# Two blocks on one core: an early table load, the split of the router's logits, and where sums of squares are issued

## The chip, the cores and the metric

The program runs on one core of one Trainium2 chip. A core has a matrix engine (TensorE, PE), a vector engine (VectorE, DVE), a scalar engine (ScalarE, ACT), a general engine (GpSimd, POOL) and a synchronising engine (SyncE, SP) that issues most transfers. Engines run side by side, each one in the order of its own instruction list, and wait for one another by semaphores. ScalarE and GpSimd issue transfers from their own lists too. The metric is device time in microseconds of one launch; shown is the median of three runs. One execution with a profile is looked at beside it.

## The reference, cut to what matters

256 tokens of width 1024 go through two blocks in float32.

- Block 1 has two layers. Each: x += (gated sum of a dilated attention and a convolution branch with layer norm and silu) @ w_out; then x += mixture of experts: `lg = h @ w_rg`, `le = h @ w_re` (4 groups of 8 experts: the best group, in it the best two experts per token), `silu(h @ w_gate[e]) * (h @ w_up[e]) @ w_down[e]`; then x += sigmoid(rms_norm(x) @ w_ple_gate) * (p @ w_ple_proj). In front of each part x is normalised: `x * rsqrt(mean(x*x) + 1e-6) * g`. At the end of block 1 comes a last such norm.
- Block 2 has one layer. It begins with `rmsnorm(x) @ w_in`, whose first columns u go through a causal convolution of four taps, then through block-diagonal products (gates of a linear recurrence); the gated linear unit, an attention with compressed, selected and windowed keys, and an MLP follow.

Since the scale of a norm is one number per token, the kernel multiplies with it late: it transposes x at once, multiplies by the gain g only, and applies the root of the mean square to the products.

## The kernel before, in words

**Tiles and numbers.** x lies in the on-chip memory as two tiles of 128 tokens by 1024. A weight block of 128 rows by 1024 comes from memory into one of four buffers (raw); ScalarE rounds it to the matrix engine's short format (whi, L304), VectorE subtracts to get the rest (wlo, L272), in one of three buffers each; PE multiplies the parts in three products (L267). Activations are split in the same way. Sums lie in eight banks, four of them for such products, four for other uses (aux).

**Turns.** `turn` (L398) transposes x for some of its eight groups of 128 channels by PE (L405) and copies the result with the gain: either to a plain tile, one group by VectorE (L410) and one by ScalarE (L412), or split in two parts, by ScalarE (L414) and VectorE (L415). `self.turned` is the last transpose.

**Sums of squares.** `sq_part` (L356) has ScalarE square a piece of x and add it up (L367), for each of the two token tiles. `ssq` and `rstd` add the pieces (L374, L353) and take the power -1/2 on GpSimd (L354). `row_sb` (L388) spreads such a root over all partitions: VectorE makes dg (L384), PE multiplies it, ScalarE copies it to rB (L390).

**Route.** In `route` the logits of a layer's 36 outputs are summed over eight groups k of channels (L697). `logits(range(KR))` is issued as it stands; the rest only behind `self.turned`, the last transpose. With KR = 2 the first two groups are issued ahead. Then comes the selection on VectorE (L704 to L721), and the gathering of tokens.

**Expert tail.** The last experts' outputs are added to x in five chunks of channels (`CHUNKS`, L911); behind each chunk stands a turn with norm_ple's gain, and, when 256 columns are done, the sum of squares of these (L984). `ple_k` multiplies the turned groups by w_ple_gate. `after` (from L998) takes tanh of the products with the root rh as scale (L1010), multiplies (L1011), adds to x (L1013), and turns x with the next norm's gain for the layer that follows. Behind this loop x is multiplied by the last norm's gain in layer 1 (yf, L1027), and both x and yf are squared and summed (L1028, `final_norm`).

**Start of block 2.** u's product is drained by VectorE, which multiplies by rB (L1139) and convolves (L1140, L1142). Since the recurrence wants another split over partitions, each pair of channel groups goes out to memory from ScalarE's list (sx, L1149 and L1154) and comes back in (xr, L1163), also from ScalarE's list, one transfer for each of four blocks; ScalarE and VectorE split xr (xh and xl, L280, L281) and PE multiplies. ScalarE's other work there: the casts of the next weight blocks (L304), tanh for gelu of the second gate (L1211, yg) and its table.

**What sets the order.** A list scheduler orders each engine's instructions by a simulated timeline (`schedule_with_timeline_sim`). `tc.issue_after(i)` holds instructions made inside it until i has been placed. A DMA issued from an engine's list waits behind what stands in front of it there.

Of the kernel before, what the change touches and what calls it, by code (L numbers as in the profile page):

```python
# [11 lines left out]
F32 = mybir.dt.float32  # L12
# [3 lines left out]
AF = mybir.ActivationFunctionType  # L16
# [5 lines left out]
P = 128  # L22
# [25 lines left out]
RING0, RING1 = 15, 20  # L48

BG, BGH = 4, 5  # L50
KR = 2
NG1 = 2
NY = 1
RQ = lambda nc: nc.scalar
# [164 lines left out]
class Kern:  # L219
# [178 lines left out]
    def turn(self, src, gcol, dst=None, kps=(0, 1, 2, 3), kds=None):  # L398

        nc = self.nc  # L400
        for kds in [kds] if kds else [(2 * kp, 2 * kp + 1) for kp in kps]:
            ps = self.ps(self.aux)
            for j, kd in enumerate(kds):
                for tt in range(2):
                    self.turned = nc.tensor.transpose(ps[:, j * T + tt * P:j * T + (tt + 1) * P], src[:, tt, kd * P:(kd + 1) * P], self.ident)  # L405
            for j, kd in enumerate(kds):
                pj, g = ps[:, j * T:(j + 1) * T], self.vec[:, gcol + kd:gcol + kd + 1]
                if dst is not None:
                    if j == 0:
                        nc.vector.tensor_scalar_mul(dst[:, kd, :], pj, g)  # L410
                    else:
                        nc.scalar.activation(dst[:, kd, :], pj, AF.Copy, scale=g)  # L412
                else:
                    nc.scalar.activation(self.hT[0][:, kd, :], pj, AF.Copy, scale=g)  # L414
                    nc.vector.scalar_tensor_tensor(self.hT[1][:, kd, :], pj, g, self.hT[0][:, kd, :].bitcast(F32),  # L415
                                                   op0=ALU.mult, op1=ALU.subtract)


    def setup(self):
        nc, a, cp = self.nc, self.a, self.cp  # L420
        self.x = cp.tile([P, 2, D], F32, name="x")
        xs = a["x"][0].rearrange("(t p) d -> p t d", p=P)
        for i in range(4):
            nc.sync.dma_start(self.x[:, :, i * 256:(i + 1) * 256], xs[:, :, i * 256:(i + 1) * 256])
        cst = cp.tile([P, C_COLS], F32, name="cst")
        nc.scalar.dma_start(cst[:, :2 * P], a["consts"][:, :2 * P])
        self.vec = cp.tile([P, a["vec"].shape[1]], F32, name="vec")
        nc.scalar.dma_start(self.vec, a["vec"])
        self.cst = cst
        self.ident = cst[:, C_ID:C_ID + P]  # L430
        self.J = cst[:, C_J:C_J + P]
        self.cos = cst[:, C_COS:C_COS + T]
        self.sin = cst[:, C_SIN:C_SIN + T]
        self.mask = cst[:, C_MASK:C_MASK + 3 * P]
        self.tri = cst[:, C_TRI:C_TRI + P]
        self.ones = cst[:, C_ONE:C_ONE + P]
        self.iota = cst[:, C_IOTA:C_IOTA + CAP]
        self.iota1 = cst[:, C_IOTA + 1:C_IOTA + 1 + CAP]
        self.act_h = lambda j, k: self.hT[j][:, k, :]
        self.nhalf = cp.tile([P, 32], F32, name="nhalf")  # L440
        nc.vector.memset(self.nhalf, -0.5)
        self.ones512 = cp.tile([P, P], F32, name="ones512")
        nc.vector.memset(self.ones512, 1.0 / 512.0)
        self.rv = cp.tile([RW, a["rv"].shape[1]], F32, name="rv")
        self.nv = cp.tile([P, a["nv"].shape[1]], F32, name="nv")
        self.spc = cp.tile([RW, 5, RC], F32, name="spc")

        g = VEC["norm_mix_2", 0]
        gf = VEC["norm_final", 0]
        nc.vector.tensor_tensor(self.vec[:, g:g + KD], self.vec[:, g:g + KD], self.vec[:, gf:gf + KD], op=ALU.mult)  # L450

        for l in range(DEPTH):
            w0 = VEC["w_dw", l]
            nc.vector.tensor_scalar_mul(self.vec[:, w0:w0 + 4 * CK], self.vec[:, w0:w0 + 4 * CK], 0.5)
            g0 = VEC["ln_conv_g", l]
            nc.vector.tensor_scalar_mul(self.vec[:, g0:g0 + 8], self.vec[:, g0:g0 + 8], 0.5)
# [213 lines left out]
    def route(self, l, mp):  # L670
# [25 lines left out]
        def logits(ks):  # L696
            for k in ks:  # L697
                for tt in range(2):
                    self.mm(pls[tt][:, :36], self.xT[:, k, tt * P:(tt + 1) * P], wr[:, k, :], k == 0, k == KD - 1)
        logits(range(KR))  # L700
        with self.tc.issue_after(self.turned.ins):
            logits(range(KR, KD))
        for tt in range(2):
# [209 lines left out]
    def moe_ple(self, l):  # L913
        nc, tc, a = self.nc, self.tc, self.a
        self.npiece, self.gates, self.ny = 0, (), 0
        with tc.tile_pool(name=f"m1_{l}", bufs=1) as mp:
# [7 lines left out]
            def ple_k(kks, after=None):  # L924
                last = None
                for hf in range(2):
                    kp = kks[0] // 2
                    if (kp, hf) not in wvs:
                        wvs[kp, hf] = self.wload(("w_ple_gate", l, hf * 512, 2 * kp), 2)
                    wv = wvs[kp, hf]  # L930
                    with tc.issue_after(last.ins) if after and last else ExitStack():
                        for tt in range(2):
                            for kk in kks:
                                for n, (j, i) in enumerate(((0, 0), (0, 1), (1, 0))):
                                    last = self.mm(pss[hf][tt], self.hT[j][:, kk, tt * P:(tt + 1) * P], wv[i][:, kk % 2, :],
                                                   kk == 0 and n == 0, kk == KD - 1 and n == 2)
                    if after is not None:
                        after(hf, last)
# [34 lines left out]
            c0, prev = 0, None  # L973
            for i, cw in enumerate(CHUNKS):
                kds = range(c0 // P, (c0 + cw) // P)
                self.quad_out(hds, c0, cw, self.aux)
                if i == 0:

                    self.new_hT(self.slot)
                    pss.extend([self.ps() for i in range(2)] for j in range(2))  # L980
                self.turn(self.x, VEC["norm_ple", l], kds=kds)
                c0 += cw
                if c0 % 256 == 0:
                    self.sq_part(c0 // 256 - 1, self.x, c0 - 256, 256)  # L984

                if prev is not None:
                    ple_k(prev)
                prev = kds
# [32 lines left out]
            for hf in range(2):  # L1021
                for c in range(2):
                    n = 512 * (2 * hf + c)
                    xs = self.x[:, :, n // 2:n // 2 + 256]
                    if end:

                        nc.vector.tensor_tensor(self.yf[:, :, n // 2:n // 2 + 256], xs, self.gf[:, n // 2:n // 2 + 256].unsqueeze(1).to_broadcast([P, 2, 256]), op=ALU.mult)  # L1027
                self.sq_part(hf, self.x, hf * 512, 512)  # L1028
            if end:
                ssx = self.ss  # L1030
                for hf in range(2):
# [550 lines left out]
```

## Time and profile before

| what | us |
|---|---|
| median of 3 runs | 1885.41 |
| lowest, highest | 1883.4, 1886.54 |
| profiled execution | 1890.22 |
| its span | 1888.3 |
| PE busy | 1588.2 (84%) |
| VectorE busy | 850.1 (45%) |
| ScalarE busy | 581.9 (31%) |
| GpSimd busy | 58.3 (3%) |
| mean granted clock of PE | 0.917 of full |

The span is read by stages. Layer 0's mixer runs to 197 us and its route to 206; the experts' weights are then streamed, to about 640; tail and layer 1's mixer follow to 855, layer 1's experts to 1300, the tail to 1345, and block 2 to the end. Busy shares are means over stages that have different limits, so the rows below are taken from single places.

### The profile page before, as it was taken

The numbers are of one execution on the slowest core, as the hardware profiler recorded it, in microseconds if no ns is written. First come the engines' busy times: TensorE is split into PE (matmuls) and PEld (weight loads), VectorE is DVE, ScalarE is ACT, GpSimd is POOL, SyncE is SP. The second block draws the span as 40 slices with busy tenths as digits, with TensorE's granted clock in tenths as the row PEclk, the third lists the DMA queues.
The fourth block names the chain that finished last, engine by engine and source line by source line (L and its number), as shares of the span: only waits on it lengthen the run. The fifth ranks groups of instructions, "written<-read, shape, count | busy, mean of one in ns | idle before, by whom it ended". The sixth has DMA issues, their size and how long they took to land. (4 is left out here: it accounts for less than half of the span.)

```text
span 1888.3 us, 27944 instructions
## 1 busy us (share of the span) xinstructions
PE 1588.2 (84%) x11259; PEld 1069.2 (57%) x11259; DVE 850.1 (45%) x1752; ACT 581.9 (31%) x1041; POOL 58.3 (3%) x74
## 2 busy tenths in 40 slices
PE   8998986666666989988866757769889989999999
PEld 8798531121212688984311212226889668799987
DVE  8986321111100279872101111002889667666643
ACT  4455110001000254651100010003565346445532
POOL 0100000000000002000000000000010100000000
PEclk9999898887888999999988768889899989999999
DMA  7657899999999956688999999998557533255654
GB/s 284 218 184 276 334 424 427 427 425 426 427 426 427 373 178 225 198 297 333 426 426 427 425 426 427 427 427 346 172 176 237 185 104 112 74 189 186 192 192 131
DMA packets 109724, 567.27 MB, mean 300 GB/s; under 512 B 12106, under 2 KB 21258, under 8 KB 61712
## 3 DMA queue, kind: packets, MB, share of 16 engines
q1 hardware_dynamic: 102976, 558.45, 76.3%
q10 hardware_dynamic: 5984, 5.82, 1.0%
q8 instruction: 93, 1.52, 0.3%
q0 software_dynamic: 624, 1.09, 0.2%
q14 instruction: 47, 0.39, 0.1%
HBM read 561.48 MB, written 3.83 MB: 299 GB/s over the span
## 5 line engine op out<-in xcount | busy, mean ns | idle before, releaser
L267 PE MATMUL ps<-mw,h 128*32 128x512 f32 x2032 | 317.1, 724 | 139.9 <-DMA mw<-in_w_exp_up_dram 71.9
L304 ACT CAST whi<-raw 128x1024 fp32r<-128x1024 f32 (+3 forms) x286 | 295.5, 1035 | 451.4 <-PE ps L267 232.6
L272 DVE TENSOR_TENSOR wlo<-raw,whi 128x1024 fp32r<-128x1024 f32 (+3 forms) x286 | 344.4, 1207 | 197.0 <-ACT whi L304 183.3
L267 PE MATMUL ps<-h,whi 128*128 128x256 f32 x2208 | 295.2, 284 | 9.8 <-ACT h L414 6.3
L267 PEld LDWEIGHTS ps<-h,whi 128*128 128x128 f32 x2208 | 275.0, 191 | 15.9 <-ACT h L414 8.1
L267 PEld LDWEIGHTS ps<-mw,h 128*32 128x32 f32 x2032 | 49.9, 118 | 346.2 <-DMA mw<-in_w_exp_up_dram 169.4
L267 PE MATMUL ps<-mw,mw 128*32 128x512 f32 (+3 forms) x1584 | 146.7, 474 | 43.9 <-DMA mw<-in_w_exp_down_dram 38.2
L267 PE MATMUL ps<-h,wlo 128*128 128x256 f32 x1104 | 151.5, 279 | 0.0
L267 PEld LDWEIGHTS ps<-h,wlo 128*128 128x128 f32 x1104 | 138.4, 187 | 0.4
L911 DVE TENSOR_TENSOR x<-x,ps 128x512 f32<-128x512 f32 (+2 forms) x60 | 34.6, 582 | 223.4 <-PE ps L267 223.4
L846 ACT ACTIVATE mw<-ps 128x512 f32<-128x512 f32 x16 | 9.6, 597 | 405.4 <-PE ps L267 405.4
L847 DVE TENSOR_TENSOR mw<-mw,ps 128x512 f32<-128x512 f32 x16 | 11.0, 687 | 263.4 <-issue 139.9
L267 PEld LDWEIGHTS ps<-mw,mw 128*32 128x32 f32 (+1 forms) x1584 | 47.2, 115 | 129.3 <-DMA mw<-in_w_exp_down_dram 76.0
L509 DVE SCALAR_TENSOR_TENSOR mw<-mw,vec,mw 128x231 f32<-128x231 f32 (+26 forms) x240 | 107.3, 500 | 0.0
L267 PE MATMUL ps<-whi,h 128*128 128x512 f32 (+1 forms) x512 | 104.5, 347 | 0.7 <-DVE h L281 0.3
L819 DVE TENSOR_TENSOR h<-ps,vec 128x256 f32<-128x256 f32 (+1 forms) x80 | 29.7, 371 | 166.9 <-PE ps L267 166.9
L267 PEld LDWEIGHTS ps<-h,h 128*128 128x128 f32 x512 | 67.8, 204 | 58.4 <-issue 50.6
L267 PE MATMUL ps<-mw 128*128 128x512 f32 (+4 forms) x328 | 88.3, 440 | 14.2 <-ACT mw L905 14.2
L267 PEld LDWEIGHTS ps<-whi,h 128*128 128x128 f32 x512 | 80.5, 192 | 15.8 <-issue 1.9
L267 PE MATMUL ps<-h,h 128*128 128x128 f32 x512 | 78.3, 299 | 9.5 <-DVE h L807 9.5
L905 ACT COPY mw<-ps 128x512 f32<-128x512 f32 (+2 forms) x50 | 21.6, 432 | 203.7 <-PE ps L267 203.7
L267 PEld LDWEIGHTS ps<-mw 128*128 128x128 f32 (+1 forms) x328 | 44.9, 196 | 58.0 <-ACT mw L905 34.1
(337 smaller groups left out, 1771.1 us busy)
## 6 DMA issues: line engine op xcount, KB each, us to landing
mw<-in_w_exp_gate_dram SPq DMA_DIRECT2D x128, 1024.0 KB, 19.6
mw<-in_w_exp_up_dram SPq DMA_DIRECT2D x126, 1024.0 KB, 19.6
mw<-in_w_exp_down_dram SPq DMA_DIRECT2D x118, 1024.0 KB, 19.6
raw<-in_w_in_dram SPq DMA_DIRECT2D x129, 512.0 KB, 4.3
raw<-in_w_mlp_in_dram SPq DMA_DIRECT2D x32, 512.0 KB, 4.3
raw<-in_w_mlp_out_dram SPq DMA_DIRECT2D x32, 512.0 KB, 4.3
raw<-in_w_out_dram SPq DMA_DIRECT2D x24, 512.0 KB, 3.7
raw<-in_w_ple_gate_dram SPq DMA_DIRECT2D x16, 512.0 KB, 16.8
```

Source lines behind the costliest of these rows:

```text
L267: return self.nc.tensor.matmul(out, lhsT, rhs, start=start, stop=stop)
L272: self.nc.vector.tensor_tensor(lo, src, hi.bitcast(F32), op=ALU.subtract)
L304: nc.scalar.copy(hv, raw[ps, :n])
L509: nc.vector.scalar_tensor_tensor(cacc[:, c, d:], u[:, c, :T - d], w, cacc[:, c, d:], op0=ALU.mult, op1=ALU.add)
L819: nc.vector.tensor_tensor(xg[:, k:k + n, :], ps[:, :n * P].rearrange("p (k s) -> p k s", k=n), self.vec[:, gcol + k:gcol + k + n].unsqueez ...
L846: nc.scalar.activation(sg, G, AF.Silu)
L847: nc.vector.tensor_tensor(sg, sg, U, op=ALU.mult)
L905: nc.scalar.copy(ys[i], Y[:, :dw])
L911: nc.vector.tensor_tensor(xs, xs, pc[:, :dw], op=ALU.add)
```

## The change

Four edits. A one-column tile `warm` is filled by a tanh on ScalarE right behind the setting of nhalf, in front of the first copies. KR goes from 2 to 6. The last ScalarE copy of a turn is kept as `self.turned_a`, and the sums of squares in the expert tail (L984 of before) and at the layer's end (L1028, for x; those of yf follow in program order) are issued behind it. Line numbers of the changed kernel are 2 higher from `setup` on, 3 to 4 behind the expert tail (L1010 is L1013 there, L1149 is L1153, L1163 is L1167, L1211 is L1215).

```diff
--- before.py
+++ after.py
@@ -48,7 +48,7 @@
 RING0, RING1 = 15, 20
 
 BG, BGH = 4, 5
-KR = 2
+KR = 6
 NG1 = 2
 NY = 1
 RQ = lambda nc: nc.scalar
@@ -411,7 +411,7 @@
                     else:
                         nc.scalar.activation(dst[:, kd, :], pj, AF.Copy, scale=g)
                 else:
-                    nc.scalar.activation(self.hT[0][:, kd, :], pj, AF.Copy, scale=g)
+                    self.turned_a = nc.scalar.activation(self.hT[0][:, kd, :], pj, AF.Copy, scale=g)
                     nc.vector.scalar_tensor_tensor(self.hT[1][:, kd, :], pj, g, self.hT[0][:, kd, :].bitcast(F32),
                                                    op0=ALU.mult, op1=ALU.subtract)
 
@@ -439,6 +439,8 @@
         self.act_h = lambda j, k: self.hT[j][:, k, :]
         self.nhalf = cp.tile([P, 32], F32, name="nhalf")
         nc.vector.memset(self.nhalf, -0.5)
+        warm = cp.tile([P, 1], F32, name="warm")
+        nc.scalar.activation(warm, self.nhalf[:, 0:1], AF.Tanh)
         self.ones512 = cp.tile([P, P], F32, name="ones512")
         nc.vector.memset(self.ones512, 1.0 / 512.0)
         self.rv = cp.tile([RW, a["rv"].shape[1]], F32, name="rv")
@@ -981,7 +983,8 @@
                 self.turn(self.x, VEC["norm_ple", l], kds=kds)
                 c0 += cw
                 if c0 % 256 == 0:
-                    self.sq_part(c0 // 256 - 1, self.x, c0 - 256, 256)
+                    with tc.issue_after(self.turned_a.ins):
+                        self.sq_part(c0 // 256 - 1, self.x, c0 - 256, 256)
 
                 if prev is not None:
                     ple_k(prev)
@@ -1025,7 +1028,8 @@
                     if end:
 
                         nc.vector.tensor_tensor(self.yf[:, :, n // 2:n // 2 + 256], xs, self.gf[:, n // 2:n // 2 + 256].unsqueeze(1).to_broadcast([P, 2, 256]), op=ALU.mult)
-                self.sq_part(hf, self.x, hf * 512, 512)
+                with tc.issue_after(self.turned_a.ins):
+                    self.sq_part(hf, self.x, hf * 512, 512)
             if end:
                 ssx = self.ss
                 for hf in range(2):
```

On PE at the route of layer 0 the logits (`ps<-wr`, two for each of eight groups) and the transposes of the last turn (L405, of x) stood in this order before:

```order
L405 MATMUL ps_2201<-cst,x 128x128
L267 MATMUL ps_2241<-wr,h_224_1974 128x36
L267 MATMUL ps_2242<-wr,h_224_1974 128x36
L267 MATMUL ps_2241<-wr,h_224_1974 128x36
L267 MATMUL ps_2242<-wr,h_224_1974 128x36
L405 MATMUL ps_2201<-cst,x 128x128 x3
L267 MATMUL ps_2241<-wr,h_224_1974 128x36
L267 MATMUL ps_2242<-wr,h_224_1974 128x36
```
After the change the first transpose and six logits stand ahead of this piece:

```order
L267 MATMUL ps_2243<-wr,h_224_1976 128x36
L267 MATMUL ps_2244<-wr,h_224_1976 128x36
L267 MATMUL ps_2243<-wr,h_224_1976 128x36
L267 MATMUL ps_2244<-wr,h_224_1976 128x36
L267 MATMUL ps_2243<-wr,h_224_1976 128x36
L405 MATMUL ps_2203<-cst,x 128x128 x3
L267 MATMUL ps_2244<-wr,h_224_1976 128x36
L267 MATMUL ps_2243<-wr,h_224_1976 128x36
```
The three later transposes went from the fifth place behind the first one to the twelfth.

On ScalarE at the end of layer 1's tail there stood before: copies of the last turns (L414), the scaling of x (L1051), casts of block 2's first weights (whi) and the copy rB:

```order
L414 ACTIVATE h_2326_14299<-ps_14341,vec 128x256
L414 ACTIVATE h_2326_14299<-ps_14355,vec 128x256
L1051 ACTIVATE x<-mw_14292,r_14386 128x1024
L304 CAST whi_14539<-raw_14537 128x1024
L414 ACTIVATE h_2326_14299<-ps_14341,vec 128x256
L414 ACTIVATE h_2326_14299<-ps_14355,vec 128x256
L304 CAST whi_14581<-raw_14579 128x1024
L390 COPY rB_14409<-ps_14411 128x256
```
After the change, in the same place, the squares of x and yf (L367) lie between the casts, and rB comes behind seven casts where it was behind two (the first of the seven stands ahead of this piece, with three squares between):

```order
L304 CAST whi_14583<-raw_14581 128x1024
L367 ACTIVATE junk_14382,ss_14379<-mw_14294 128x512
L304 CAST whi_14613<-raw_14611 128x1024
L1055 ACTIVATE x<-mw_14294,r_14388 128x1024
L367 ACTIVATE junk_14384,ss_14379<-mw_14294 128x512
L304 CAST whi_14655<-raw_14653 128x1024
L367 ACTIVATE junk_14386,ss_14379<-mw_14294 128x512
L304 CAST whi_14685<-raw_14683 128x1024
L304 CAST whi_14727<-raw_14725 128x1024
L304 CAST whi_14757<-raw_14755 128x1024
L390 COPY rB_14411<-ps_14413 128x256
```
The copies L414 all stand in front of these rows now, and rB behind the casts of five more weight blocks.

On ScalarE at the start of block 2, before, transfers sx (out) and xr (in) stood between the casts of u's last weight blocks:

```order
L304 CAST whi_14797<-raw_14795 128x1024
L1149 DMA sx<-W_14429 128x2x256
L304 CAST whi_14839<-raw_14837 128x1024
L304 CAST whi_14869<-raw_14867 128x1024
L304 CAST whi_14905<-raw_14903 112x1008
L1149 DMA sx<-W_14429 128x2x256
L304 CAST whi_14911<-raw_14909 112x1008
L1163 DMA xr<-sx 112x3x256
L1211 ACT_TABLE_LOAD
L1211 ACTIVATE yg<-yg 64x256
L304 CAST whi_14998<-raw_14996 112x1008
L280 CAST xh_14899<-xr 112x768
```
After the change:

```order
L304 CAST whi_14799<-raw_14797 128x1024
L304 CAST whi_14841<-raw_14839 128x1024
L304 CAST whi_14871<-raw_14869 128x1024
L304 CAST whi_14907<-raw_14905 112x1008
L304 CAST whi_14913<-raw_14911 112x1008
L304 CAST whi_15000<-raw_14998 112x1008
L1215 ACT_TABLE_LOAD
L1215 ACTIVATE yg<-yg 64x256
L1153 DMA sx<-W_14431 128x2x256 x2
L1167 DMA xr<-sx 112x3x256
L1153 DMA sx<-W_14431 128x2x256
L280 CAST xh_14901<-xr 112x768
```
Two sx transfers and xr moved behind all these casts, the table load and the activation that writes yg.

## Rows read from the trace of the kernel before

**Rows 1.** Page, busy time, share of the span and instructions of one engine.
```profile
PE 1588.2 (84%) x11259; PEld 1069.2 (57%) x11259; DVE 850.1 (45%) x1752; ACT 581.9 (31%) x1041; POOL 58.3 (3%) x74
```

**Rows 2.** Windows: length, busy time of five engines, granted clock, DMA share, GB/s.
```profile
202.00:212.00 10.00, 7.49 (x33) 4.26 (x33) 5.37 (x33) 2.33 (x7) 0.49 (x1) 0.50 0.43 163
300.00:350.00 50.00, 33.77 (x190) 8.15 (x194) 5.12 (x10) 2.36 (x4) 0.00 (x0) 0.83 1.01 427
673.00:680.00 7.00, 6.82 (x32) 5.99 (x30) 4.36 (x13) 3.63 (x10) 0.70 (x1) 0.51 0.23 75
1328.00:1338.00 10.00, 6.20 (x27) 5.91 (x28) 8.11 (x19) 7.45 (x20) 0.70 (x1) 0.52 0.32 105
```

**Rows 3.** Chain of waits, 1340 to 1400 us: start, duration, what.
```profile
1366.89 5.19 DMA sx<-W
...
1372.10 5.66 DMA xr<-sx
...
1377.79 4.26 DMA sx<-W
...
1382.07 3.67 DMA xr<-sx
```

**Rows 4.** Timeline of PE, 1371 to 1380 us: start, duration, instruction, idle before.
```profile
1378.66 0.98 PE L267 MATMUL ps<-xh,whi 112*112 112x256 f32 x3 [5.22 <-ACT xh L280]
```

**Rows 5.** Timeline of ScalarE (ACT), 0 to 16 us.
```profile
5.65 1.28 ACT L414 ACT_TABLE_LOAD   x1 [5.65 <-DMA vec<-in_vec_dram]
...
8.14 1.57 ACT L414 ACTIVATE h<-ps,vec 128x256 fp32r<-128x256 f32 x4 [0.36 <-DVE h L415]
```

**Rows 6.** Timeline of PE, 196 to 214 us.
```profile
198.73 2.77 PE L267 MATMUL ps<-wr,h 128*128 128x36 f32 x24
204.51 1.89 PE L267 MATMUL ps<-A,cst 128*128 128x64 f32 x8 [3.02 <-issue]
```

**Rows 7.** Timeline of ScalarE, 196 to 214 us.
```profile
199.45 0.47 ACT L412 ACTIVATE h<-ps,vec 128x256 f32<-128x256 f32 x1 [1.09 <-DVE h L410]
```

**Rows 8.** Timeline of ScalarE, 661 to 676 us.
```profile
662.24 0.42 ACT L367 ACTIVATE junk<-x 128x256 f32<-128x256 f32 x1 [1.40 <-DVE x L911]
...
663.19 0.46 ACT L414 ACTIVATE mw<-ps,vec 128x256 fp32r<-128x256 f32 x1
...
666.61 1.06 ACT L304 CAST whi<-raw 128x1024 fp32r<-128x1024 f32 x1
```

**Rows 9.** Waits of PE, 660 to 676 us: total, times, longest, by releaser.
```profile
PE ps L405 <- DVE x L1013: 2.2, 2, 1.2
PE ps L267 <- ACT h L414: 2.0, 1, 2.0
PE ps L267 <- ACT mw L414: 1.0, 1, 1.0
```

**Rows 10.** Waits of PE, 1320 to 1336 us.
```profile
PE ps L267 <- ACT h L414: 4.3, 2, 2.3
```

**Rows 11.** Timeline of all engines, 809 to 824 us.
```profile
809.84 1.66 PE L267 MATMUL ps<-mw,whi 128*128 128x256 f32 x12
810.95 1.41 DVE L540 TENSOR_TENSOR mw<-mw,ps 128x256 f32<-128x256 f32 x4
...
816.89 5.43 PE L267 MATMUL ps<-mw,whi 128*128 128x256 f32 x33 [4.45 <-ACT mw L280]
```

**Rows 12.** Timeline of ScalarE, 1340 to 1375 us.
```profile
1343.09 0.38 ACT L390 COPY rB<-ps 128x256 f32<-128x256 f32 x1 [0.48 <-PE ps L267]
...
1355.58 1.06 ACT L304 CAST whi<-raw 128x1024 fp32r<-128x1024 f32 x1 [1.77 <-PE ps L267]
...
1369.75 1.04 ACT L304 CAST whi<-raw 112x1008 fp32r<-112x1008 f32 x1 [1.83 <-PE ps L267]
...
1372.47 1.28 ACT L1211 ACT_TABLE_LOAD   x1 [1.67 <-DMA sx<-W]
1373.76 0.41 ACT L1211 ACTIVATE yg<-yg 64x256 f32<-64x256 f32 x1
```

## The prediction

> **What bounds the kernel now.** Read first the page's busy table: PE is busy 84% of the span [rows 1], so ask where it is not. The table of windows answers by stage [rows 2]: in the expert stage (300 to 350 us) the DMA share is 1.01 at 427 GB/s and PE is busy 33.77 of 50 us, so there the weights' transfers bound, and whatever delays the route in front of them is paid in full. In three short stretches (202 to 212, 673 to 680, 1328 to 1338 us) the granted clock is 0.50 to 0.52, the lower level of 1.2 GHz. They follow waits at the route and at the two layers' ends. Then read the timelines of those places for what each wait is for, and last the chain of waits around 1370 us, which passes through ScalarE's queue (transfer sx, transfer xr, a split) while PE has a gap of 5.22 us [rows 3, 4]. From 1398 us on PE is nearly dense to the end, so what the start of block 2 loses stays lost.
>
> The profiled execution took 1890.22 us (span 1888.3); the median of the three runs is 1885.41. I work out differences in the profiled one and put them on the median. A measurement of this kernel tells 0.2%, or 3.8 us, from no change.
>
> **ScalarE's table loaded at once.** Before, the load starts at 5.65 us behind the vector DMA and takes 1.28 us; the copies of the first turn follow it. The third copy (8.14) then waits 0.36 us for VectorE's L415 [rows 5]. VectorE subtracts what ScalarE has copied and is what the next turns wait for, and the transposes wait for x itself. So at most 1.28 us is gained at the head, and nothing where x and VectorE come last; the reload that a later function needs stays. Bounds -1.3 to +0.3; I take 0, since the row nearest to it shows ScalarE waiting. The Trainium skill (ScalarE: Activation LUTs, "What ACT_TABLE_LOAD costs") prices a switch at about 2.66 us, load and drain together. By it the gain could be 2.7 us; the row shows 1.28, and the sum keeps to the row.
>
> **Logits of six groups in front of the last turn.** The order of instructions shows the last three transposes behind eleven logit products where it was four; the amount of work on PE is the same. 24 products (12 rows of the order, two records each) take 2.77 us, 0.115 us each, without a wait [rows 6]: they cover the copies L410 and L412. Seven rows more in front are 14 products, 1.6 us, so L412 starts at 199.45 + 1.6 = 201.05, takes 0.47 us [rows 7], and the four products that need it end at about 202.1, where the last ended at 201.50. That is +0.6 us. The selection that follows is one chain on VectorE, PE idles 3.02 us meanwhile [rows 6], and then come the gathers that let the expert weights flow. The layers are alike, so +1.3 us. Bounds 0 (if the copy's delay is covered) to +2.6.
>
> **Squares behind the turns' copies, expert tail.** In four of five chunks no instruction waits for the squares: 0. In the last, the copy L414 stands behind two squares (662.24 to 663.19) and PE waits for it 1.0 us [rows 8, 9]. It may now start some 0.4 us earlier. The squares that were in front of it come behind it, and with them the root that L1010 needs; the order also puts a cast in front of L1010, 1.06 us for one of its form, so L1010 starts about 0.7 us later, and the x updates (L1013) after it. The eight copies of norm_mix's turns are then free of squares. PE's waits are 1.0 us for the first copy, 2.2 for L1013 and 2.0 for the later copies in layer 0, and 4.3 for the later copies in layer 1 [rows 9, 10]. The first shrinks by 0.4; those for L1013 grow by the 0.7 that L1010 loses; those for the later copies shrink by the squares that went ahead of them, about 1 us in a tail, but only as far as L1013 lets the transposes come. I take +0.3 for both layers together, bounds -3 (two squares of 1.05 us and the 0.4, in both layers) to +3 (L1013 late by 0.7 at each of its four steps).
>
> **Squares behind the copies, start of layer 1.** The root of the new norm (rB) is ready some 5 us later, since it now stands behind casts that wait for PE. In the convolution's norm the order shows dg's products some 20 PE rows later. Twelve such products took 1.66 us, 0.138 us each, so 2.8 us. L540, which reads dg's products, began at 810.95 although they were through by about 810.1; that slack gives back 0.8. PE's wait of 4.45 us at the end of this chain [rows 11] grows by 2.0. Bounds -1 (chain lands elsewhere) to +3.
>
> **Squares behind the copies, start of block 2.** This is the largest term. The trace has ScalarE's instructions in their written order, and its casts wait for PE to free a buffer: the one at 1369.75 came after an idle wait of 1.83 us for PE and took 1.04, so one cast comes every 2.87 us [rows 12]. Before, the copy rB ran at 1343.09, in front of these casts; now the squares of x and yf sit between the casts, and rB stands behind the cast that ran at 1355.58 in before. So rB comes at about 1356.6, 13 us late, and VectorE's convolution (L1139 and after) starts at about 1357.4. It can catch up between its subtractions. But the order also sends the transfers sx (two, the second at 1366.89) behind all six casts that are left, the table load and yg. The last cast can't start before 1369.75 + 2.87 = 1372.6; add 1.04, 1.28 and 0.41 [rows 12] and the sx transfers are issued at about 1375.3, where the second was at 1366.89 [rows 3]: 8.4 us later. From there the chain is the one of before: sx 5.19 and xr 5.66 us, or 4.26 and 3.67 as its second pair shows [rows 3], and 0.9 from xr's end to PE. So PE gets its operand at 1375.3 + 7.93 + 0.9 = 1384.1 at best, or 1375.3 + 10.85 + 0.9 = 1387.0, against 1378.66 [rows 4]: +5.5 to +8.4. I take +7. It is paid in full: PE's amount behind it is unchanged, and nothing else is ready in its queue. If VectorE has not caught up by 1375, the later chunks add more (the third rival). Least 0, if the casts find their buffers early.
>
> **The sum.** 0 + 1.3 + 0.3 + 2.0 + 7.0 = +10.6 us, 0.56%. On the median 1896.0; the profiled execution would be about 1900.8.
>
> **Rivals.**
> *The half-clock stretches go.* If copies that come sooner keep PE from going idle at the two tails, the 7 and 10 us at half clock [rows 2] give back half of themselves, 8.5 us, and the later sx chain stays hidden: 1885.4 - 8.5 = about 1877. For it speaks that PE waits for L414 four times there, 7.3 us together [rows 9, 10], which is what the change removes. Against it: each of these copies waits for x updates (L1013), and these come later. The Trainium skill (TensorE: Matmul & The Clock Gate, "HAM oscillation") takes the cost of a throttled time at half of it, as the 8.5 us does. Chance 15%.
> *The transfers have cover.* The squares move but the casts before sx pass early (ScalarE is free to run ahead if the raw blocks land sooner), so sx is no later than xr needs, and PE starts as before at 1378.7. What is left is the route and the norm: +1.3 + 0.3 + 2.0 = +3.6 at most, without the norm's part +1.6: about 1887. For it: ScalarE idles 1.83 us ahead of a cast, so it has time to spare. Against it: that wait is for PE, not for data [rows 12]. Chance 18%.
> *VectorE becomes the bound.* rB is 13 us late, and all of u's convolution waits for it. If VectorE catches none of it up, xr and with it PE's restart come 13 us later, at 1391.7, in place of the 7: +13 + 3.6 = +16.6, 1902. This decides from the point at which the convolution's end, and no longer ScalarE's queue, is the later of the two. For it: L1139 stands at the head of every u group. Against it: the sums have four buffers, and VectorE waits for ScalarE's casts between its subtractions, so it can make up most of it by 1375. Chance 12%, in the same direction as the forecast.
> *Forecast* as summed: 55%.
>
> **How the numbers follow.** Slower by over 0.2% (above 1889.2): forecast 55 and the VectorE bound 12, 67%. Within 0.2%: the covered transfers, 18%. Faster (below 1881.6): 15%. The likeliest case alone spans 1892 to 1900. The range reaches below to 1882, past the covered case, and above to 1902, the price of the third; what is left out is nearly all of the first rival and a little above.
>
> **What would show it.** Right: in the timeline of ScalarE around 1375 us the sx transfers stand behind the table load, PE's gap there is 11 to 14 us, and rB is copied at about 1356. The last logits end 0.6 us later than before. The wait at the convolution's norm is about 6.4 us. Wrong: sx issued by 1370 us (the order did not hold it), or the clock at 1328 to 1338 us at its higher level (first rival), or PE idle within u's projection, 1343 to 1372 us (VectorE's bound).

## The result, and the profile after

The changed kernel takes 1915.74 us (median of 4 runs, 1913.94 to 1918.07) against 1884.41 us for the kernel before: ratio 1.0152, 95% interval 1.0133 to 1.0171, some 29 us slower by this ratio (the two medians alone lie 31.3 us apart). Forecast were 1896.0 us and a range of 1882 to 1902: the direction came true, the size did not, 10.6 us against some 29.

The time is best divided at instructions that both traces have. The table gives the time between such places on PE (us), for the profiled execution of before, a second profiled execution of before (c_before), the changed kernel, and the changed kernel with the addresses of before (e5_after_ring, below).

| from, to | before | before again | after | addresses of before |
|---|---|---|---|---|
| start to the selection's product (A) of layer 0's route | 204.51 | 204.29 | 205.00 | 206.75 |
| to the last product with w_ple_gate (expert stage) | 462.26 | 462.08 | 468.37 | 460.63 |
| to A of layer 1's route (tail, mixer) | 195.51 | 197.34 | 198.69 | 197.45 |
| to the last product with w_ple_gate (expert stage) | 462.89 | 463.50 | 467.43 | 463.27 |
| to the end of u's projection (tail, start of block 2) | 48.27 | 48.29 | 47.87 | 47.17 |
| to the transposes of the compressed keys | 165.35 | 165.03 | 174.53 | 171.15 |
| to the end | 349.51 | 349.77 | 353.41 | 353.98 |

The two executions of before differ by up to 1.8 us in such a stretch. So 10.7 us of the 27 between the profiled executions come in the two expert stages, to which the prediction gave no term; 9.2 between u and the keys, where it said 7; 3.9 in the last stage; the rest is small. The window of the expert stage that [rows 2] showed at 427 GB/s, and the stretches at half clock (columns as there):

```profile
300.00:350.00 50.00, 31.62 (x181) 6.75 (x174) 3.25 (x6) 2.36 (x4) 0.00 (x0) 0.83 1.01 419
676.00:683.00 7.00, 5.69 (x23) 4.70 (x24) 6.84 (x14) 3.55 (x7) 0.00 (x0) 0.51 0.41 143
683.00:690.00 7.00, 7.00 (x62) 7.00 (x60) 2.62 (x6) 5.67 (x13) 0.66 (x1) 1.00 0.08 7
1343.00:1353.00 10.00, 8.88 (x43) 7.89 (x44) 9.29 (x19) 4.88 (x12) 0.00 (x0) 0.55 0.22 68
```

The DMA share is again 1.01, but the same bytes move at 419 GB/s. The half-clock stretches have not gone: they stand behind the tails' waits as before.

The issues of the weights' transfers (source, engine, count, KB, median us to landing), before:

```profile
mw<-in_w_exp_gate_dram SPq DMA_DIRECT2D x128, 1024.0 KB, 19.6
```
and after:

```profile
mw<-in_w_exp_gate_dram SPq DMA_DIRECT2D x128, 1024.0 KB, 19.9
```
A transfer of 1 MB takes 0.3 us longer from issue to landing, 1.5%, and with the DMA share at 1.01 the stage goes at the pace of these transfers.

The route on PE, which answers to [rows 6]:

```profile
197.24 2.62 PE L267 MATMUL ps<-wr,h 128*128 128x36 f32 x22
199.69 0.52 PE L405 MATMUL ps<-cst,x 128*128 128x128 f32 x3
200.05 0.31 PE L267 MATMUL ps<-wr,h 128*128 128x36 f32 x2
200.79 1.19 PE L267 MATMUL ps<-wr,h 128*128 128x36 f32 x8 [0.43 <-DVE h L410]
205.00 1.89 PE L267 MATMUL ps<-A,cst 128*128 128x64 f32 x8 [3.02 <-issue]
```
The transposes stand behind 22 logit records, PE waits 0.43 us for the copy L410, and A comes 0.5 us later although the first logits came 0.24 us earlier.

The start of block 2 on ScalarE, which answers to [rows 12]:

```profile
1370.36 0.37 ACT L390 COPY rB<-ps 128x256 f32<-128x256 f32 x1 [0.33 <-PE ps L267]
...
1387.06 1.03 ACT L304 CAST whi<-raw 112x1008 fp32r<-112x1008 f32 x1 [2.47 <-DMA raw<-in_gate_a_w_dram]
1388.11 1.28 ACT L1215 ACT_TABLE_LOAD   x1
1389.40 0.41 ACT L1215 ACTIVATE yg<-yg 64x256 f32<-64x256 f32 x1
1390.92 2.94 ACTq L1153 DMA_DIRECT2D sx<-W  x2
1397.73 0.34 ACTq L1167 DMA_DIRECT2D xr<-sx  x1
...
1401.87 0.83 ACT L280 CAST xh<-xr 112x768 fp32r<-112x768 f32 x1 [12.05 <-DMA xr<-sx]
```
and PE, which answers to [rows 4]:

```profile
1402.76 0.98 PE L267 MATMUL ps<-xh,whi 112*112 112x256 f32 x3 [15.40 <-ACT xh L280]
```
rB comes 13.0 us after its place of before, if the 14.3 us by which the whole stage is late are taken off (1343.09 and 14.3). The sx transfers stand behind the table load and yg, as forecast, and PE's gap is 15.40 us where it was 5.22. The second execution of before has a shorter gap still:

```profile
1377.23 0.63 PE L267 MATMUL ps<-xh,whi 112*112 112x256 f32 x3 [1.73 <-DVE W L1142]
```
There PE waits another 3.25 us soon after, and the stage is as long (165.03 and 165.35 us in the table), so the gap itself is not the price; the table's stage is. Now look at the time between yg's end (1389.81) and the transfers (1390.92): when sx went out, ScalarE had been ready for 1.1 us. VectorE in the same stretch:

```profile
1371.19 2.08 DVE L1143 TENSOR_TENSOR ur<-ps,rB 128x256 f32<-128x256 f32 x6
1373.18 1.38 DVE L1144 TENSOR_SCALAR W<-ur,nv 128x256 f32<-128x256 f32 x4
...
1387.59 0.42 DVE L1143 TENSOR_TENSOR ur<-ps,rB 64x256 f32<-64x256 f32 x1
...
1389.62 1.27 DVE L1146 SCALAR_TENSOR_TENSOR W<-ur,nv,W 128x256 f32<-128x256 f32 x3
...
1392.96 1.67 DVE L1146 SCALAR_TENSOR_TENSOR W<-ur,nv,W 128x256 f32<-128x256 f32 x4
```
From 1371.19 on VectorE drains u and convolves. The steps that end at 1390.9 release the first sx transfer; the second step of those from 1392.96 on releases the second, at 1393.5, and the first xr waits for that one. In the chain of waits the last links are VectorE's convolution, then sx, then xr:

```profile
1389.62 0.55 DVE W L1146 x2
...
1390.41 0.48 DVE W L1146
1390.89 0.65 DVE W L1144 x2
...
1391.93 1.12 DVE wlo L272
...
1393.48 4.18 DMA sx<-W
...
1397.73 4.12 DMA xr<-sx
...
1401.87 0.84 ACT xh L280
```

### The profile page after: what moved, and what is told of

The parts are those of the page before. It is cut to its first block, busy times and chain, and to the rows that moved or that the text cites. A ratio compares the mean times of both kernels' runs of the same rounds, so it can differ in the third digit from the quotient of the medians.

```text
span 1915.3 us, 27933 instructions
## 1 busy us (share of the span) xinstructions
PE 1598.6 (83%) x11259; PEld 1075.9 (56%) x11259; DVE 850.7 (44%) x1752; ACT 583.0 (30%) x1042; POOL 56.6 (3%) x74
## 5 line engine op out<-in xcount | busy, mean ns | idle before, releaser
L267 PE MATMUL ps<-mw,h 128*32 128x512 f32 x2032 | 322.8, 734 | 142.7 <-DMA mw<-in_w_exp_up_dram 75.4
L511 DVE SCALAR_TENSOR_TENSOR mw<-mw,vec,mw 128x255 f32<-128x255 f32 (+29 forms) x240 | 106.6, 498 | 0.0
L267 PE MATMUL ps<-mw 128*128 128x512 f32 (+4 forms) x328 | 86.4, 431 | 14.3 <-ACT mw L907 14.3
## 6 DMA issues: line engine op xcount, KB each, us to landing
mw<-in_w_exp_gate_dram SPq DMA_DIRECT2D x128, 1024.0 KB, 19.9
mw<-in_w_exp_up_dram SPq DMA_DIRECT2D x126, 1024.0 KB, 19.9
mw<-in_w_exp_down_dram SPq DMA_DIRECT2D x118, 1024.0 KB, 19.9
```

What stands on the lines that cost most here:

```text
L267: return self.nc.tensor.matmul(out, lhsT, rhs, start=start, stop=stop)
L511: nc.vector.scalar_tensor_tensor(cacc[:, c, d:], u[:, c, :T - d], w, cacc[:, c, d:], op0=ALU.mult, op1=ALU.add)
```

## The experiments

Each kernel was run beside the kernel before on the same chip. Of each edit only the lines that matter are shown, for e2 and e5 against the changed kernel and for the others against before. Theory 1: the tile `warm` takes 32 bytes, every later tile is allocated 32 bytes on, and the weights' transfers land at addresses that suit them less. Its rivals: the order of the instructions, or the single execution, set the rate. Theory 5: the start of block 2 is bound by VectorE, since rB is late; its rival is the prediction's, ScalarE's list.

**e1_pad32: the addresses alone.**

```diff
         nc.vector.memset(self.nhalf, -0.5)
+        cp.tile([P, 1], F32, name="pad")
```


> The kernel before, with one tile of 4 bytes that nothing reads or writes, allocated where the change puts warm. It takes a slot of 32 bytes, so that every later tile starts 32 bytes on (the expert weights' buffers at 102944 instead of 102912); the order of the instructions is that of before. Theory 1 (the places of the tiles set the rate): the weights land in 19.9 us instead of 19.6 and move at 419 instead of 427 GB/s, which is 13 us over the two expert stages, and the matmuls of the last stages take 116 instead of 112 ns, 3 us: 1900, +16 us. Rival 2 (the rate belongs to the order of the changed kernel or to that one execution): 427 GB/s and the time of before, within 0.2%.

Measured: 1.0079 (1.0051 to 1.0108), about +15 us, with the instruction order of before on every engine. The weights' transfers:

```profile
mw<-in_w_exp_gate_dram SPq DMA_DIRECT2D x128, 1024.0 KB, 19.9
```
The expert stages (table's second and fourth line) took 469.45 and 469.10 us, 13.4 us more than in before; the last stage 3.6 us more. Theory 1 holds: an unused tile alone brings half of the change's cost. Rival 2 falls. Which of the shifted tiles matters was not taken apart; the stage's bytes are nearly all weights.

**e2_after_64: the changed kernel, shifted by 64 bytes.**

```diff
-        warm = cp.tile([P, 1], F32, name="warm")
-        nc.scalar.activation(warm, self.nhalf[:, 0:1], AF.Tanh)
+        warm = cp.tile([P, 16], F32, name="warm")
+        nc.scalar.activation(warm[:, 0:1], self.nhalf[:, 0:1], AF.Tanh)
```


> The changed kernel with warm 64 bytes wide, so that every later tile starts 64 bytes on and none sits at an odd multiple of 32. Theory 1: 427 GB/s again, what remains is the order: about +11 us on before (route 1, tails and norm 1 to 2, start of block 2 10), 1895 to 1897. Rival 2: as the changed kernel, 1915.

Measured: 1.0127 (1.0101 to 1.0154), +24 us. The expectation that 64 bytes would be as good as none was wrong:

```profile
300.00:350.00 50.00, 34.96 (x173) 7.10 (x166) 3.24 (x6) 2.35 (x4) 0.00 (x0) 0.72 1.01 421
```
421 GB/s, between the two. In before the weights' buffers start at 102912, a multiple of 512; here at 102976. (These addresses are counted from the program, as in what was expected of e1; no profile shows them.)

**e5_after_ring: the changed kernel at the addresses of before.**

```diff
-        warm = cp.tile([P, 1], F32, name="warm")
-        nc.scalar.activation(warm, self.nhalf[:, 0:1], AF.Tanh)
+        warm = self.sm.tile([P, 4, 2], F32, tag="ss", name="warm")
+        nc.scalar.activation(warm[:, 0, 0:1], self.nhalf[:, 0:1], AF.Tanh)
```


> The changed kernel, its instructions in the same order; only warm takes its 32 bytes from the ring of the small sums (ss), so that every later tile has its address of before (weights' buffers at 102912). Theory 1 (addresses): 427 GB/s, 19.6 us for a weight, and the sum of the order's parts, +14 us, about 1902. Rival 2 (the changed order itself slows the transfers): 419 GB/s, 1915.

Measured: 1.0058 (1.0038 to 1.0078), 1899.0 us, +11 us. The instructions stand in the order of the changed kernel; the rate is that of before:

```profile
300.00:350.00 50.00, 32.82 (x184) 7.33 (x178) 3.98 (x8) 2.35 (x4) 0.00 (x0) 0.83 1.01 427
```
So the change's 29 us are about 11 of order (7 to 15 by the interval) and 18 of addresses.

**e3_sq_end: the squares at the layers' end alone.**

```diff
-                self.sq_part(hf, self.x, hf * 512, 512)
+                with tc.issue_after(self.turned_a.ins):
+                    self.sq_part(hf, self.x, hf * 512, 512)
```


> Before, with only the squares at a layer's end (L1028) issued behind the turns' copies; no table load, KR 2. Theory 1 with the start of block 2 as the main cost of the order: PE's gap there 12 to 15 us instead of 5.2, and in all +8 to +11 us. Rival 3 (the gap comes from the later arrival that route and tail bring): gap as before, +0 to +2.

Measured: 1.0074 (1.0048 to 1.0100), +14 us. PE's gap at the start of block 2:

```profile
1389.33 0.98 PE L267 MATMUL ps<-xh,whi 112*112 112x256 f32 x3 [16.39 <-ACT xh L280]
```
In this trace yg ends at 1374.8 on ScalarE, and the first two sx are issued at 1378.0 and 1380.9, so here too ScalarE's list is ready first. Within the intervals this edit has all of the order's cost.

**e6_sq_end_l0: the same in layer 0 only.**

```diff
+                with ExitStack() if end else tc.issue_after(self.turned_a.ins):
```


> Before, with the squares at the layer's end behind the copies in layer 0 only. Theory: PE's wait at the convolution's norm goes from 4.45 to 5.7 us and the layer's end moves by about as much: +1 to +3 us. Rival (half of the +14 of both layers is here): +7.

Measured: 1.0014 (1.0003 to 1.0025), +2.6 us. PE's wait at the convolution's norm is as long as in the changed kernel (5.75 us; before 4.45 [rows 11]):

```profile
817.33 5.97 PE L267 MATMUL ps<-mw,whi 128*128 128x256 f32 x31 [5.74 <-ACT mw L280]
```
By difference, the rest of e3's 14 us is layer 1's end.

**e7_sq_end_pool: the transfers of block 2's start from another list.**

```diff
-RQ = lambda nc: nc.scalar
+RQ = lambda nc: nc.gpsimd
```
(on top of e3_sq_end)

> Before, with the squares at the layers' end behind the copies, and the transfers sx, xr, sh of block 2 issued from GpSimd's list instead of ScalarE's. Theory 5 (VectorE bounds the start of block 2 once rB is late; ScalarE's list has no part in it): PE's gap stays at 14 to 17 us, the time within 0.2% of the same squares with ScalarE's list, +12 to +16. Rival 6 (sx stands behind casts and table in ScalarE's list, as predicted): the gap falls to 5 to 9 us, the time to +3 to +7.

Measured: 1.0085 (1.0068 to 1.0101), +16 us. GpSimd's list, which does nothing else there, waits for VectorE (idle before, and for what, in brackets):

```profile
1377.00 0.77 POOL L1150 DMA_DIRECT2D sx<-W  x1 [26.28 <-DVE W L1143]
1379.95 1.52 POOL L1150 DMA_DIRECT2D sx<-W  x2 [2.18 <-DVE W L1143]
1382.32 0.72 POOL L1150 DMA_DIRECT2D sx<-W  x1 [0.86 <-DVE W L1143]
1384.02 1.41 POOL L1164 DMA_DIRECT2D xr<-sx  x2 [0.97 <-DMA sx<-W]
```
and PE's gap is as long as with ScalarE's list:

```profile
1388.38 0.98 PE L267 MATMUL ps<-xh,whi 112*112 112x256 f32 x3 [16.74 <-ACT xh L280]
```
Theory 5 holds, and the prediction's reason falls. GpSimd's issues are longer than ScalarE's (0.7 to 0.8 us for one against 0.3 to 0.5), which may be part of what keeps the gap; it can't explain the waits of 26.28 and 2.18 us for VectorE.

**e4_kr_sq_tail, e8_sq_tail, e9_kr, e10_warm_ring: the other edits.** KR 6 and the expert tail's squares together; the squares alone; KR alone; the table load alone, its tile in the ring as in e5.

```diff
-KR = 2
+KR = 6
...
-                    self.sq_part(c0 // 256 - 1, self.x, c0 - 256, 256)
+                    with tc.issue_after(self.turned_a.ins):
+                        self.sq_part(c0 // 256 - 1, self.x, c0 - 256, 256)
```


> Before, with KR 6 and the squares of the expert tail issued behind the copies, without the other two edits. Theory: +1.3 us from the route, 0 to +2 from the tail: +1 to +3, within 0.2%. Rival 4 (these two parts are what was meant as a gain, PE's waits at the tail's end shrink): -2 to -5 us.

> Before, with only the squares of the expert tail issued behind the copies: the version that the earlier runs point to as the fastest. Theory: the tails get 1 to 2 us shorter (from the traces of the runs with this edit) and nothing else moves: -1 to -2 us, about -0.1%. Rival (the gain of the tails is given back at the next stage): 0.

> Before, with only KR 6. Theory as predicted: the last logits end 0.6 us later in each layer, all of it paid: +1 to +2 us, about +0.1%. Rival (the expert stage absorbs it): 0.

> Before, with only the early table load, its output in the ring of the small sums, so that all addresses are those of before. Theory as predicted: 0 to -0.3 us. Rival (the whole load of 1.28 us is gained): -1.3 us. At 0.1% these two may not come apart by the time; the first matmul of the trace tells.

Measured: 1.0003 (0.9988 to 1.0019), 0.9999 (0.9985 to 1.0014), 0.9999 (0.9989 to 1.0009) and 1.0005 (0.9991 to 1.0019). None can be told from no change, where +1 to +3, -1 to -2, +1 to +2 and 0 to -0.3 us were expected. In e4's trace the tails are 1.2 us shorter in layer 1 and each route about 1 us longer. No version was found that beats the kernel before.

**c_before: the kernel before again.**

> The kernel before once more, for a second profile: 427 GB/s and 19.6 us for a weight by every theory; PE's cadence in the last 150 us is 91 matmuls in 10 us if that belongs to the kernel, and may be 87 if it changes from one execution to the next.

Measured, in one execution: 1892.33 us, 19.6 us for a weight. The last stage keeps its pace (windows as in [rows 2]):

```profile
1735.00:1755.00 20.00, 20.00 (x179) 20.00 (x178) 13.69 (x16) 11.14 (x15) 0.00 (x0) 1.00 0.54 187
```
against the changed kernel at the same work:

```profile
1757.00:1777.00 20.00, 20.00 (x173) 20.00 (x171) 12.99 (x15) 10.99 (x15) 0.00 (x0) 1.00 0.60 192
```
The count of matmuls in 20 us is that of a pace: 0.112 against 0.116 us for one. But e10_warm_ring, which adds only one table load and one tanh at the head and leaves the addresses alone, has the slower pace too:

```profile
1735.00:1755.00 20.00, 20.00 (x172) 20.00 (x171) 12.78 (x14) 11.16 (x15) 0.00 (x0) 1.00 0.52 186
```

## Why the prediction was right in direction and wrong in size

**Table load at once: the step that failed.** "I take 0", with bounds of -1.3 to +0.3 us. Of the load this was right: after the change the third copy starts at 8.11 where [rows 5] has 8.14, and waits 0.71 us for VectorE instead of 0.36:

```profile
1.75 1.28 ACT L443 ACT_TABLE_LOAD   x1 [1.75 <-issue]
...
8.11 1.57 ACT L414 ACTIVATE h<-ps,vec 128x256 fp32r<-128x256 f32 x4 [0.71 <-DVE h L415]
```
and e10_warm_ring shows no effect. But the edit also allocates a tile, and the sum had no term for that. It measures +0.79% alone (e1) and 0.94% as the difference of the changed kernel and e5, 15 to 18 us, more than all that was forecast. Most of it is the weights' transfers: the two expert stages are 925 us in before, a transfer takes 19.9 instead of 19.6 us, 1.5% more, which makes 14 us; 13.4 were measured in e1 and 10.7 in the changed kernel. [rows 2] showed where such a cost would be paid: a stage at DMA share 1.01 pays for every per cent of a transfer. That a shift of 32 bytes has a cost stood in no row. The Trainium skill (DMA: Bandwidth & Descriptors, "How a descriptor splits into AXI transactions") says that when a descriptor, one piece of a transfer, does not start at a multiple of 256 bytes, bytes ahead of its start are fetched, not used, and still paid for. That is about bytes that are read, while the edit moved the places that are written, which that section does not price. The traces agree in the direction: 427 GB/s at an address that is a multiple of 512, 419 at 32 bytes past, 421 at 64 past. They don't show that this rule is the cause: by an estimate from its count 64 past would be no better than 32.

**Route: right.** +0.6 us in each layer was forecast; A came 0.5 us later in layer 0 with 0.24 us of it made up ahead, and from the first logits to A layer 0 took 7.0 to 7.5 us in the eight profiles without this edit and 7.8 to 8.5 in the five with it. In time it can't be seen (e9_kr), so whether the expert stage pays it in full is not shown.

**Expert tail: near.** +0.3 us forecast, bounds -3 to +3; by e8_sq_tail no change that can be measured. The waits answer to [rows 9, 10]; layer 0 and layer 1 after:

```profile
PE ps L405 <- DVE x L1016: 3.4, 1, 3.4
PE ps L267 <- ACT mw L414: 0.6, 1, 0.6
PE ps L267 <- ACT h L414: 0.6, 1, 0.6
```

```profile
PE ps L405 <- DVE x L1016: 3.9, 2, 3.4
PE ps L267 <- ACT mw L414: 0.6, 1, 0.6
PE ps L267 <- ACT h L414: 0.6, 1, 0.6
```
As worked out, the wait for L1013 (here L1016) grew, to 3.4 and 3.9 us, and those for the copies shrank to 0.6 each; the forecast had the first copy's right (0.4 less) and missed how far the later ones shrink. The tail of layer 1 to the end of u's projection got 0.4 us shorter. The first rival (half-clock stretches go) fell: the stretch from 1343 us is still at 0.55.

**Start of layer 1: right, a little large.** Forecast: the wait of 4.45 us grows by 2.0. It is 5.75 us, so 1.3 more; the edit in this layer costs 2.6 us in all (e6, interval 0.6 to 4.7).

**Start of block 2: mechanism wrong, size near by luck.** Forecast +7 from ScalarE's list; this stage measured +9.2 in the changed kernel and +5.8 in e5. What held: rB 13 us late, sx behind casts, table and yg, and the time at which ScalarE is ready for sx: 1389.8, where the forecast's 1375.3 and the 14.3 us make 1389.6. What failed: "It can catch up between its subtractions". VectorE drained three pairs of groups at once, at 1371.19, and released the first sx at 1390.9 and the second at 1393.5. From rB's copy to the second sx 23.1 us passed, where it was 23.8 before [rows 3, 12]: of the 13 us VectorE made up 0.7. That is the third rival's mechanism. PE's restart came only 9.8 us later, and not 13, because the two transfers behind took 4.18 and 4.12 us instead of 5.19 and 5.66. Both lists were late by nearly the same amount, which is why the price came out near with the wrong cause, and why moving the transfers to another list (e7) gained nothing. The forecast named the sign for this (PE idle within u's projection) too narrowly: PE was not idle there, the four buffers held, and the delay showed only at xr. One thing is left open: VectorE's own list changed as well. Ahead of the first sx stood 8 of the steps that add a tap of the convolution (L1142) before and 16 (L1146) after, where a pair of groups needs 6. A VectorE list that finishes the first pair first was not tried.

**Last stage: not in the sum.** +3.9 us in the changed kernel, +3.6 in e1, +3.4 in e2, +3.7 in e3, +4.5 in e5, and 0.1 to 0.3 in c_before, e4, e6 and e7. But it is also +3.3 in e8, +3.2 in e9 and +2.2 in e10, whose times can't be told from before's; in these three the stage ahead is 2.9 to 4.4 us shorter. So the +3.9 is not shown to be a cost of the change. It is a matter of pace and not of waits, and it is not settled what sets it. The two stages together, from the end of u's projection to the end, take 512.7 to 517.8 us in the eight profiles that leave the squares at layer 1's end in place, and 525.1 to 527.9 in the five that move them: 10 to 13 us more than the 514.9 of before. This is the steadier measure of what the start of block 2 costs, and it is above the forecast's 7. That e5's 11 us for the order are so near the sum's 10.6 is therefore partly luck too.

What was said to show the forecast wrong did not come (sx by 1370, the clock at its higher level, PE idle within u's projection). Of the signs for it, PE's gap missed: 15.4 us and not 11 to 14. The larger part of what was wrong, the tile's place, lay where the prediction had not looked.

## What to carry to other kernels

An edit that allocates a tile, however small, moves all tiles behind it: where a stage is bound by transfers, compare the addresses of its buffers before and after, and give a helper tile a place that shifts nothing. When an order moves a value that many wait for (rB), follow the engine that must then do its work late, not only the list in which the next transfer stands; two lists that end within a few us of each other hide one another, and only taking one away tells which decides. And three edits out of four here (e8, e9, e10) moved instructions by 0.5 to 2 us at waits that looked worth it, and none could be measured.

## What the runs showed of the hardware

The same 1 MB transfers from memory moved at 426 or 427 GB/s in the window from 300 to 350 us in the ten profiles with buffers at 102912, at 419 in the two at 102944, and at 421 in the one at 102976. The two expert stages together took 923 to 926 us in the ten, 936 and 939 in the two, and 934 in the one.

The same dense run of matmuls of 128x256 goes at one of two paces, 0.112 or 0.116 us each, at full granted clock and with the weight loads busy 100%: 178 to 179 or 172 to 173 in 20 us. Neither the addresses nor the order explain it: before, c_before, e4, e6 and e7 have the faster pace, and e3, e5, e8, e9 and e10 the slower one at the same addresses, e10 with nothing moved. Before showed the faster pace in both of its profiles; no other kernel was profiled twice, so whether the pace changes from one execution to the next is not shown. The cause is open.
